# Two column tiles begun at a stage boundary, remainders last, and priority for the rows' transposes and splits

## The chip, the cores and the metric

The kernel runs on one core of a Trainium2 chip. The metric is the device time of one execution in microseconds (us). Three runs of the kernel before are shown, and one further execution was recorded by the profiler; span, windows and timelines are of that one. The engines are TensorE (PE, with its weight loads as PEld), VectorE (DVE), ScalarE (ACT), GpSimd (POOL) and SyncE (SP, which issues DMAs).

## The reference

One layer of a decoder step for a prompt of 1024 tokens (`D_MODEL` 1024) and for 8 sample rows with a paged cache of 8192 tokens each. The lines that the boundaries below compute:

```python
xp = xp + merge_heads(fox_prompt(q, k, v, logf), sgu_prompt(u, z, w_s[l], b_s[l]), ..., w_o[l])
xp = xp + cross_attend(rmsnorm(xp, g_cross[l]), mk, mv, w_cq[l], w_co[l])
f, conv_p = conv_ffn(rmsnorm(xp, g_ffn[l]), ..., w_up[l], conv_w[l], conv_b[l], w_down[l])
xp = xp + f
```

`cross_attend` begins with `xn @ w_cq`, `conv_ffn` with `xn @ w_up` (5632 columns). The sample rows go through the same layer, with attention over the cache (`fox_sample`).

## The kernel before

All data is float32. A product of two matrices is made of three matmuls per 128-row block of the contraction: each operand is split into a rounded part ("h") and a remainder ("l"), and `gemm3` (lines 268 to 274) issues h.h (L272), then the stationary h with the moving l (L273), then the stationary l with the moving h (L274). `split` makes the two parts: ACT copies (with a per-partition gain) into the rounded part (L238; L235 for weights), DVE subtracts it from the source for the remainder (L239; L236 for weights). `wload` fetches a piece of weight through SP and splits it; there are 4 raw buffers, 4 for remainders and 5 for rounded parts.

The prompt goes through the late stages in two halves of 512 tokens: merge and output projection, cross-attention, MLP. These are called mid0, ffn0, mid1 and ffn1 (`prompt`, L1830). At each of the two boundaries within a half the same thing happens:

- `out_proj` (L1014) multiplies by the last weight of the stage before (w_o, or w_co). It makes the first 512 columns of all four row blocks, then the second 512 columns in three groups: row block 0, row block 1, and row blocks 2 and 3 together (48 matmuls, L1072 to L1074). `residual` (L1002) adds each result to the rows `xt` on DVE (L1006) and sums its squares on ACT (L230). For row blocks 2 and 3 that already has the scheduler's priority (`HP`).
- Ahead of the MLP each row block is also scaled by its norm's factor: a factor on ACT (L1022) and POOL (L1023), the scaling on ACT (`scaled`, L1028, for row blocks 0 and 1; `both`, L1035 and L1036, for 2 and 3, with priority). Ahead of cross-attention the rows stay unscaled, and the factor is used later.
- `norm_T` (L1089) turns the rows into columns, in two passes: tokens of row blocks 0 and 1, then of 2 and 3. A pass has four tiles of four PE transposes (L1105) and two splits each (L238, L239). After each pass `first` is called, which multiplies the half that is there. Before the change that is one column tile of 128 outputs: 24 matmuls of 256 columns into one PSUM bank, held from the first pass to the end of the second.

`cross` (L1119) goes on with the other column tiles of w_cq at 512 columns each (`products`), `ffn` (L1250) with pairs of column tiles `ft` and `ft + NF` (NF is 22; gate and value), each with its own `wload` (`up`), then a convolution on ACT and DVE.

PSUM tiles come from `BK` (L146), which deals out a pool of four banks ("ba") and one of two ("bb") in turn. Rows, rounded parts and remainders of the prompt are tiles "u" of one pool of 18.

The sample rows run in the background: the generator `sample` is advanced by one step when the prompt's steps have yielded enough (`PACE`), except while `held` is set, which it is from the last group of `out_proj` to the end of `norm_T`. A step of the key side (`kstep`, L1403) gathers cache rows by a POOL DMA (L1406) into a "kv" buffer (4 of them), multiplies on DVE (L1422) and reduces (L1426). The value side is 16 matmuls (L1474) on a gathered buffer (L1468).

The order of instructions on each engine is fixed when the program is built. The context is opened with `schedule_with_timeline_sim=True`: a scheduler goes along a modelled timeline, and of the instructions that are ready it takes the one that was traced earliest. What is traced under `tc.high_priority()` is taken before everything else that is ready. `tc.issue_after` adds an order between two instructions of an engine. On the chip each engine then works through its list.

Of the kernel before, what the change touches and what calls it, by code (L numbers as in the profile page):

```python
# [18 lines left out]
P = 128  # L19
# [59 lines left out]
def build(nc, tc, ctx, a, phases=None):  # L79
# [66 lines left out]
    def BK():  # L146
        turn_[0] += 1
        return BB() if turn_[0] % BR == BR - 1 else BA()
# [83 lines left out]
    def split(src, h, l, scale=None):  # L232

        if scale is None:
            nc.scalar.activation(h, src, AF.Copy)  # L235
            nc.vector.tensor_tensor(l, src, h.bitcast(F32), op=ALU.subtract)  # L236
        else:
            nc.scalar.activation(h, src, AF.Copy, scale=scale)  # L238
            nc.vector.scalar_tensor_tensor(l, src, scale, h.bitcast(F32), op0=ALU.mult, op1=ALU.subtract)  # L239
# [28 lines left out]
    def gemm3(out, pairs):  # L268

        n = len(pairs)  # L270
        for i, (sh, sl, mh, ml) in enumerate(pairs):
            mmul(out, sh, mh, start=(i == 0), stop=False)  # L272
            mmul(out, sh, ml, start=False, stop=False)  # L273
            mmul(out, sl, mh, start=False, stop=(i == n - 1))  # L274

    paused = [False]

# [811 lines left out]
    def norm_T(ys, g0, first):  # L1089


        hs, ls = [], []
        for t0 in (0, 2):
            c = slice(t0 * P, (t0 + 2) * P)
            if callable(ys[t0]):
                ys[t0:] = ys[t0]()
            for kk in range(0, 8, 2):
                if t0 == 0:
                    h2, l2 = U([P, 2, 512], F32R), U([P, 2, 512], F32R)
                    hs += [h2[:, 0, :], h2[:, 1, :]]  # L1100
                    ls += [l2[:, 0, :], l2[:, 1, :]]
                tr = TR()
                for q in range(2):
                    for i in range(2):
                        nc.tensor.transpose(  # L1105
                            tr[:, (q * 2 + i) * P : (q * 2 + i + 1) * P], ys[t0 + i][:, (kk + q) * P : (kk + q + 1) * P], ident
                        )
                for q in range(2):
                    k = kk + q
                    split(tr[:, q * 256 : (q + 1) * 256], hs[k][:, c], ls[k][:, c], scale=gp[:, g0 + k : g0 + k + 1])  # L1110
                yield 0.6
            first(hs, ls, c)
            if t0 == 0:
                yield 3
        held[0] = False
        return hs, ls


    def cross(xt, sq):  # L1119
# [10 lines left out]
        fetch(1)  # L1130

        ws = [wload(wpair(a["w_cq"], kk, 0, 512), 1024) for kk in range(4)]
        q2, ps0 = [], MM()

        def products(out, ws, dt_, hs, ls, c):
            cb = slice(dt_ * P, (dt_ + 1) * P)
            gemm3(
                out,
                [(ws[k // 2][0][:, k % 2, cb], ws[k // 2][1][:, k % 2, cb], hs[k][:, c], ls[k][:, c]) for k in range(8)],
            )  # L1140

        hs, ls = yield from norm_T(xt, G_CROSS, lambda hs, ls, c: products(ps0[:, c], ws, 0, hs, ls, c))
# [61 lines left out]
        for n in range(2):  # L1204
            if n:
                ws = [wload(wpair(a["w_cq"], kk, n * 512, 512), 1024) for kk in range(4)]
            for dt_ in range(4):
                if dt_ % 2 == 0:
                    q2.append(U([P, 2, 512]))
                if n or dt_:  # L1210
                    ps = MM()
                    products(ps, ws, dt_, hs, ls, slice(0, 512))
                else:
                    ps = ps0
                nc.scalar.activation(q2[-1][:, dt_ % 2, :], ps[:, :512], AF.Copy)
# [32 lines left out]
    hlast = [const.tile([P, 2 * NF, 2], F32, tag=f"hlast{h}", name=f"hlast{h}") for h in range(2)]  # L1248

    def ffn(hf, xt, ys, late=None):  # L1250
        w0, pv0 = wload(a["w_up"][0], 1024), BK()

        def up(out, w, hs, ls, c):
            hv, lv = (w[q].rearrange("p (k c) -> p k c", c=P) for q in range(2))
            gemm3(out, [(hv[:, k, :], lv[:, k, :], hs[k][:, c], ls[k][:, c]) for k in range(8)])

        hs, ls = yield from norm_T(ys, G_FFN, lambda hs, ls, c: up(pv0[:, c], w0, hs, ls, c))
        if hf:

            fix = sm([P, 2 * NF, 2], "fix", 1)  # L1260
# [8 lines left out]
        for gi, gn in enumerate(GROUPS):  # L1269
            gh, gl = [], []  # L1270
            for f in range(f0, f0 + gn):
                hc2 = []
                for part in range(2):
                    ft = f + part * NF
                    cw = [gp[:, CW + i * 44 + ft : CW + i * 44 + ft + 1] for i in range(3)]
                    cb = gp[:, CB + ft : CB + ft + 1]
                    if ft:
                        w_, pv = wload(a["w_up"][ft], 1024), BK()
                        up(pv, w_, hs, ls, slice(0, 512))
                    else:  # L1280
# [730 lines left out]
```

## Time and profile before

| what | us |
|---|---|
| runs | 1814.82, 1810.97, 1816.68; median 1814.82 |
| the profiled execution | 1810.32 |
| its span, first to last instruction | 1808.3 |
| PE busy in it | 1741.4 |
| DVE busy | 1396.9 |
| ACT busy | 734.3 |

The granted clock of TensorE is 0.989 of the full one over the span. In a timeline a row has its start, its duration, engine, line of the kernel, operation, output and input, shapes and a count; in brackets stands how long the engine was idle just before, and what ended the idle time. Matmuls are pipelined: the distance from one start to the next is what one costs, and the duration is longer. In a table of waits a row has the waiting line, what released it, the sum, the number of times and the longest. "Busy" of PE counts time with a matmul in flight, at any clock.

### The profile page before, as it was taken

How to read it: one execution, taken by the hardware profiler on the slowest of the kernel's cores; microseconds unless marked ns; L12 is line 12 of the kernel's file. 1: busy time of each engine (PE TensorE's matmuls, PEld its weight loads, DVE VectorE, ACT ScalarE, POOL GpSimd, SP SyncE). 2: the span in 40 equal slices, each digit the busy share in tenths (PEclk: the TensorE clock that was granted, in tenths of full speed). 3: DMA queues.
4: the chain of work that ended last, by engine and by line, in shares of the span. 5: the costliest groups of instructions: out<-in, count | busy, mean ns of one | idle time of the engine just before them, and what ended most of it. 6: DMA issues, size and time to landing. Idle time of an engine off the chain costs nothing.

```text
span 1808.3 us, 25094 instructions
## 1 busy us (share of the span) xinstructions
PE 1741.4 (96%) x9637; PEld 1292.1 (71%) x9637; DVE 1396.9 (77%) x1729; ACT 734.3 (41%) x1378; POOL 501.8 (28%) x461
## 2 busy tenths in 40 slices
PE   8999999878999999999999999989999999999997
PEld 5887776656676767777777776766676678767875
DVE  4689658987788887999989899888875549855344
ACT  6332265465633544433323244235453333232332
POOL 1232333432133433223332233433322111001110
PEclk9999999998999999999999999999999999999999
DMA  7886888786597986778878788979878677568982
GB/s 290 304 304 230 293 316 331 261 278 196 213 404 268 346 315 252 264 280 338 321 278 317 267 313 329 383 285 349 325 283 314 246 289 253 183 260 295 358 314 81
DMA packets 157075, 521.06 MB, mean 288 GB/s; under 512 B 20875, under 2 KB 40843, under 8 KB 124187
## 3 DMA queue, kind: packets, MB, share of 16 engines
q0 software_dynamic: 57168, 341.14, 49.6%
q1 hardware_dynamic: 92874, 165.73, 26.2%
q10 hardware_dynamic: 6912, 12.59, 1.9%
q8 instruction: 76, 1.25, 0.3%
q14 instruction: 45, 0.36, 0.1%
HBM read 495.47 MB, written 23.93 MB: 287 GB/s over the span
## 4 chain that ended last, share of the span: by engine, by line
PE 53%; issue 8%; DMA 6%; DVE 5%; POOL 2%; ACT 2%; POOLq 0%; DVEq 0%; SPq 0%; ACTq 0%
PE ba L274 7%; PE ba L272 7%; PE ba L273 7%; PE bb L273 4%; PE bb L274 4%; PE bb L272 4%; PE dv L1474 4%; DMA kv<-cache_k,io 3%; DMA kv<-cache_v,io 2%; PE dv L321 1%; PE dv L1750 1%; PE ba L1055 1%; PE ba L1054 1%; PE ba L1056 1%; DVE s L1426 1%
## 5 line engine op out<-in xcount | busy, mean ns | idle before, releaser
L235 ACT ACTIVATE wh<-wr 128x1024 fp32r<-128x1024 f32 (+2 forms) x220 | 228.6, 1044 | 490.4 <-PE ba L273 157.7
L236 DVE TENSOR_TENSOR wl<-wr,wh 128x1024 fp32r<-128x1024 f32 (+2 forms) x220 | 262.3, 1198 | 174.0 <-PE ba L274 59.3
L1406 POOL DMA_INDIRECT kv<-cache_k,io x128 | 195.0, 1523 | 562.5 <-DVE s L1426 321.1
L1422 DVE TENSOR_TENSOR kv<-kv,d 128x1024 f32<-128x1024 f32 (+1 forms) x156 | 258.0, 1680 | 29.9 <-DMA kv<-cache_k,io 29.9
L1426 DVE TENSOR_REDUCE s<-kv 128x16 f32<-128x1024 f32 (+1 forms) x156 | 258.1, 1672 | 0.1
L1468 POOL DMA_INDIRECT kv<-cache_v,io x128 | 167.4, 1308 | 276.5 <-PE dv L1474 191.0
L273 PE MATMUL ba<-u,wh 128*128 128x512 f32 (+1 forms) x560 | 219.6, 392 | 1.8 <-DVE u L239 1.5
L272 PE MATMUL ba<-u,wh 128*128 128x512 f32 (+1 forms) x560 | 219.2, 393 | 1.7 <-ACT u L238 1.7
L274 PE MATMUL ba<-u,wl 128*128 128x512 f32 (+1 forms) x560 | 218.7, 392 | 0.0
L272 PE MATMUL ba<-wh,u 128*128 128x512 f32 (+1 forms) x495 | 186.9, 379 | 1.7 <-ACT u L235 1.7
L273 PE MATMUL ba<-wl,u 128*128 128x512 f32 (+1 forms) x495 | 185.5, 375 | 1.2 <-DVE wl L236 1.2
L274 PE MATMUL ba<-wh,u 128*128 128x512 f32 (+1 forms) x495 | 183.8, 376 | 0.0
L1474 PE MATMUL dv<-kv,s 128*32 128x512 f32 x1024 | 125.0, 598 | 2.9 <-DMA kv<-cache_v,io 2.9
L273 PEld LDWEIGHTS ba<-u,wh 128*128 128x128 f32 x560 | 106.0, 189 | 30.3 <-issue 5.2
L273 PE MATMUL bb<-u,wh 128*128 128x512 f32 (+1 forms) x304 | 118.6, 390 | 8.7 <-DVE u L239 8.7
L274 PEld LDWEIGHTS ba<-u,wl 128*128 128x128 f32 x560 | 105.9, 189 | 29.1 <-issue 6.1
L272 PEld LDWEIGHTS ba<-u,wh 128*128 128x128 f32 x560 | 105.9, 189 | 28.7 <-issue 4.0
L272 PE MATMUL bb<-u,wh 128*128 128x512 f32 (+1 forms) x304 | 118.5, 390 | 0.1
L274 PE MATMUL bb<-u,wl 128*128 128x512 f32 (+1 forms) x304 | 117.6, 387 | 0.0
L272 PEld LDWEIGHTS ba<-wh,u 128*128 128x128 f32 x495 | 93.0, 188 | 26.8 <-issue 6.9
L274 PEld LDWEIGHTS ba<-wh,u 128*128 128x128 f32 x495 | 92.8, 188 | 21.5 <-issue 3.8
L273 PEld LDWEIGHTS ba<-wl,u 128*128 128x128 f32 x495 | 93.1, 188 | 20.1 <-DVE wl L236 1.9
(432 smaller groups left out, 3251.0 us busy)
## 6 DMA issues: line engine op xcount, KB each, us to landing
wr<-w_up SPq DMA_DIRECT2D x88, 512.0 KB
kv<-w_up POOLq DMA_DIRECT2D x22, 1024.0 KB
wr<-w_down SPq DMA_DIRECT2D x40, 512.0 KB
kv<-w_down POOLq DMA_DIRECT2D x11, 1024.0 KB
wr<-w_in SPq DMA_DIRECT2D x16, 512.0 KB
wr<-w_o SPq DMA_DIRECT2D x16, 512.0 KB
wr<-w_cq SPq DMA_DIRECT2D x16, 512.0 KB
wr<-w_co SPq DMA_DIRECT2D x16, 512.0 KB
```

The costliest lines, as they stand in the source:

```text
L235: nc.scalar.activation(h, src, AF.Copy)
L236: nc.vector.tensor_tensor(l, src, h.bitcast(F32), op=ALU.subtract)
L272: mmul(out, sh, mh, start=(i == 0), stop=False)
L273: mmul(out, sh, ml, start=False, stop=False)
L274: mmul(out, sl, mh, start=False, stop=(i == n - 1))
L321: mmul(ps[32 * j : 32 * j + 32, :w], xT[:, k, :] if nk == 8 else xT[:, k * 8 : k * 8 + 32], raw[:, q, j * w : (j + 1) * w], start=(k == 0) ...
L1054: mmul(pss[i], mh[k][:, tb], wh, start=(k == korder[0]), stop=False)
L1406: nc.gpsimd.indirect_dma_start(kv, None, a["cache_k"], off(kidx[:, b, ch : ch + 1]))
L1422: nc.vector.tensor_tensor(kvv[:, i : i + m, :], kvv[:, i : i + m, :], qb.unsqueeze(1).broadcast_to((P, m, 512)), op=ALU.mult)
L1426: nc.vector.tensor_reduce(s[:, ch * 4 + i : ch * 4 + i + m, :].rearrange("p k h -> p (k h)"), kvv[:, i : i + m, :].rearrange("p k (h d) -> ...
L1468: nc.gpsimd.indirect_dma_start(kv, None, a["cache_v"], off(kidx[:, b, ch : ch + 1]))
L1474: mmul(dv[32 * j : 32 * j + 32, :], s[:, ch * 4 : ch * 4 + 4, :].rearrange("p k h -> p (k h)"), kvv[:, j, :], start=(ch == 1), stop=(ch == ...
```

## The change

Three things are changed. `gemm3_late` is new: it takes several products and issues for all of them first the matmuls that need the rounded part of the moving operand (h.h, and stationary l with moving h), and after these the ones that need its remainder. `first` in `cross` and in `ffn` now begins two column tiles and not one: tiles 0 and 1 of w_cq, and tiles 0 and 22 of w_up (whose second weight is loaded ahead of `norm_T`). The later loops skip what has been begun. And in `norm_T` the transposes and splits of both passes are traced under `tc.high_priority()`.

```diff
+    def gemm3_late(outs):
+
+        for out, pairs in outs:
+            for i, (sh, sl, mh, ml) in enumerate(pairs):
+                mmul(out, sh, mh, start=(i == 0), stop=False)
+                mmul(out, sl, mh, start=False, stop=False)
+        for out, pairs in outs:
+            for i, (sh, sl, mh, ml) in enumerate(pairs):
+                mmul(out, sh, ml, start=False, stop=(i == len(pairs) - 1))
...
                 tr = TR()
-                for q in range(2):
-                    for i in range(2):
-                        nc.tensor.transpose(
...
-                for q in range(2):
-                    k = kk + q
-                    split(tr[:, q * 256 : (q + 1) * 256], hs[k][:, c], ls[k][:, c], scale=gp[:, g0 + k : g0 + k + 1])
+                with tc.high_priority():
+                    for q in range(2):
+                        for i in range(2):
+                            nc.tensor.transpose(
...
+                    for q in range(2):
+                        k = kk + q
+                        split(tr[:, q * 256 : (q + 1) * 256], hs[k][:, c], ls[k][:, c], scale=gp[:, g0 + k : g0 + k + 1])
...
-        q2, ps0 = [], MM()
+        q2, begun = [], [MM() for _ in range(2)]
...
+        def first(hs, ls, c):
+            gemm3_late([(ps[:, c], pairs(ws, d, hs, ls, c)) for d, ps in enumerate(begun)])
+
+        hs, ls = yield from norm_T(xt, G_CROSS, first)
...
-                if n or dt_:
+                if n or dt_ >= len(begun):
                     ps = MM()
-                    products(ps, ws, dt_, hs, ls, slice(0, 512))
+                    gemm3(ps, pairs(ws, dt_, hs, ls, slice(0, 512)))
                 else:
-                    ps = ps0
+                    ps = begun[dt_]
...
-        w0, pv0 = wload(a["w_up"][0], 1024), BK()
+        begun = {ft: (wload(a["w_up"][ft], 1024), BK()) for ft in (0, NF)}
...
+        def first(hs, ls, c):
+            gemm3_late([(pv[:, c], pairs(w, hs, ls, c)) for w, pv in begun.values()])
+
+        hs, ls = yield from norm_T(ys, G_FFN, first)
...
-                    if ft:
+                    if ft in begun:
+                        pv = begun.pop(ft)[1]
+                    else:
                         w_, pv = wload(a["w_up"][ft], 1024), BK()
-                        up(pv, w_, hs, ls, slice(0, 512))
-                    else:
-                        pv = pv0
+                        gemm3(pv, pairs(w_, hs, ls, slice(0, 512)))
```

More of the change, by code (lines that the diff above doesn't have):

```diff
@@ L1102, in norm_T @@
                 tr = TR()
-                for q in range(2):
-                    for i in range(2):
-                        nc.tensor.transpose(
-                            tr[:, (q * 2 + i) * P : (q * 2 + i + 1) * P], ys[t0 + i][:, (kk + q) * P : (kk + q + 1) * P], ident
-                        )
-                for q in range(2):
-                    k = kk + q
-                    split(tr[:, q * 256 : (q + 1) * 256], hs[k][:, c], ls[k][:, c], scale=gp[:, g0 + k : g0 + k + 1])
+                with tc.high_priority():
+                    for q in range(2):
+                        for i in range(2):
+                            nc.tensor.transpose(
+                                tr[:, (q * 2 + i) * P : (q * 2 + i + 1) * P], ys[t0 + i][:, (kk + q) * P : (kk + q + 1) * P], ident
+                            )
+                    for q in range(2):
+                        k = kk + q
+                        split(tr[:, q * 256 : (q + 1) * 256], hs[k][:, c], ls[k][:, c], scale=gp[:, g0 + k : g0 + k + 1])
                 yield 0.6
@@ L1132, in cross, with pairs @@
         ws = [wload(wpair(a["w_cq"], kk, 0, 512), 1024) for kk in range(4)]
-        q2, ps0 = [], MM()
-        def products(out, ws, dt_, hs, ls, c):
+        q2, begun = [], [MM() for _ in range(2)]
+        def pairs(ws, dt_, hs, ls, c):
             cb = slice(dt_ * P, (dt_ + 1) * P)
[L1137 to L1142, printed above, removed]
+            return [(ws[k // 2][0][:, k % 2, cb], ws[k // 2][1][:, k % 2, cb], hs[k][:, c], ls[k][:, c]) for k in range(8)]
+        def first(hs, ls, c):
+            gemm3_late([(ps[:, c], pairs(ws, d, hs, ls, c)) for d, ps in enumerate(begun)])
+        hs, ls = yield from norm_T(xt, G_CROSS, first)
         r = rows_rstd(sq, 0, 4)
@@ L1250, in ffn, with pairs @@
     def ffn(hf, xt, ys, late=None):
-        w0, pv0 = wload(a["w_up"][0], 1024), BK()
-        def up(out, w, hs, ls, c):
+        begun = {ft: (wload(a["w_up"][ft], 1024), BK()) for ft in (0, NF)}
+        def pairs(w, hs, ls, c):
             hv, lv = (w[q].rearrange("p (k c) -> p k c", c=P) for q in range(2))
-            gemm3(out, [(hv[:, k, :], lv[:, k, :], hs[k][:, c], ls[k][:, c]) for k in range(8)])
-        hs, ls = yield from norm_T(ys, G_FFN, lambda hs, ls, c: up(pv0[:, c], w0, hs, ls, c))
+            return [(hv[:, k, :], lv[:, k, :], hs[k][:, c], ls[k][:, c]) for k in range(8)]
+        def first(hs, ls, c):
+            gemm3_late([(pv[:, c], pairs(w, hs, ls, c)) for w, pv in begun.values()])
+        hs, ls = yield from norm_T(ys, G_FFN, first)
         if hf:
```

## The prediction

> **What bounds the kernel now.** I read the page first, then the waits of TensorE over the part that the change can touch, then the windows of the four boundaries, and last the timelines inside them. A boundary here is a call of norm_T: into cross-attention (cross) and into the gated MLP (ffn), once for each half of the prompt.
>
> ```profile
> span 1808.3 us, 25094 instructions
> PE 1741.4 (96%) x9637; PEld 1292.1 (71%) x9637; DVE 1396.9 (77%) x1729; ACT 734.3 (41%) x1378; POOL 501.8 (28%) x461
> ...
> PE bb L273 <- DVE u L239: 8.7, 5, 5.5
> ...
> PE ba L272 <- ACT u L238: 1.7, 3, 0.9
> ...
> PE ba L273 <- DVE u L239: 1.5, 1, 1.5
> ...
> PE ba L1105 <- ACT u L1035: 1.1, 1, 1.1
> ```
>
> TensorE (PE) is busy 96% of the span, so only its idle 67 us and the time it runs at a lower clock can be won without taking work away. Between 500 and 1400 us its longest waits are the four lines above: a product with the remainder waits for the remainder's subtraction (L273 for L239), a product for the rounded part (L272 for L238), a transpose for a scaled row (L1105 for L1035). All belong to the boundaries. The windows (columns: length, PE busy, PEld, DVE, ACT, POOL, granted clock, DMA share, GB/s) give the sums: in order cross 0, ffn 0, cross 1, ffn 1, and then the three stretches with a low clock.
>
> ```profile
> core 0: us, PE busy (x) PEld busy (x) DVE busy (x) ACT busy (x) POOL busy (x), PEclk, DMA share, GB/s
> 545.00:565.00 20.00, 17.27 (x115) 13.78 (x114) 19.24 (x32) 9.07 (x22) 5.68 (x5) 0.91 0.92 362
> 702.00:718.00 16.00, 12.61 (x75) 10.60 (x74) 11.90 (x26) 12.38 (x31) 3.80 (x4) 0.89 0.95 385
> 1177.00:1204.00 27.00, 20.96 (x133) 16.13 (x132) 24.90 (x36) 9.78 (x22) 10.51 (x8) 0.87 0.73 263
> 1340.00:1359.00 19.00, 17.45 (x118) 14.79 (x120) 11.14 (x23) 12.23 (x30) 1.35 (x3) 1.00 0.39 159
> ...
> 559.00:564.00 5.00, 4.63 (x22) 3.75 (x21) 5.00 (x8) 0.47 (x1) 0.11 (x1) 0.66 1.04 409
> 705.00:714.00 9.00, 6.15 (x33) 5.55 (x34) 5.67 (x14) 7.27 (x19) 2.11 (x3) 0.81 1.01 421
> 1188.00:1195.00 7.00, 5.89 (x29) 5.89 (x30) 6.23 (x12) 1.55 (x4) 2.49 (x2) 0.54 0.47 159
> ```
>
> Idle: 2.73 + 3.39 + 6.04 + 1.55 = 13.7 us. Lost to the clock, as busy time times the missing share: 4.63 x 0.34 + 6.15 x 0.19 + 5.89 x 0.46 = 1.6 + 1.2 + 2.7 = 5.5 us. Together **19.2 us** is all that the boundaries hold.
>
> Why PE stands is seen in the largest gap, first PE and then VectorE (DVE):
>
> ```profile
> 1177.48 0.39 PE L1074 MATMUL ba<-wh,u 128*128 128x512 f32 x1
> ...
> 1180.59 0.60 PE L1105 MATMUL bb<-cp,u 128*128 128x128 f32 x4
> 1181.03 1.04 PE L1105 MATMUL ba<-cp,u 128*128 128x128 f32 x8
> ...
> 1189.11 0.58 PE L273 MATMUL bb<-u,wh 128*128 128x256 f32 x1 [5.50 <-DVE u L239]
> ```
>
> ```profile
> 1167.33 0.68 DVE L1006 TENSOR_TENSOR u<-bb,u 128x512 f32<-128x512 f32 x1
> ...
> 1177.22 1.39 DVE L1006 TENSOR_TENSOR u<-ba,u 128x512 f32<-128x512 f32 x2 [1.03 <-PE ba L1074]
> ...
> 1184.41 0.86 DVE L239 SCALAR_TENSOR_TENSOR u<-ba,gp,u 128x256 fp32r<-128x256 f32 x2
> 1185.19 1.20 DVE L1426 TENSOR_REDUCE s<-kv 128x16 f32<-128x1024 f32 x1
> 1186.32 2.35 DVE L1422 TENSOR_TENSOR kv<-kv,d 128x1024 f32<-128x1024 f32 x2
> 1188.59 0.47 DVE L239 SCALAR_TENSOR_TENSOR u<-ba,gp,u 128x256 fp32r<-128x256 f32 x1
> ```
>
> The background's key products (L1422, L1426) stand in DVE's order ahead of the remainder that PE wants, for 3.4 us here (1185.19 to 1188.59). They were traced before norm_T, so the scheduler preferred them. And the rows are there early: row block 1 is complete at 1168.0, 9.5 us before the last out_proj matmul at 1177.48, yet its transposes come after that matmul, because they are traced after it.
>
> The gain counts one for one only if the prompt's own work ends last. It does:
>
> ```profile
> 1783.66 0.31 SPq L1804 DMA_DIRECT2D o_ys<-vsum  x1
> 1795.25 8.61 SPq L1340 DMA_DIRECT2D o_y<-u  x5
> ```
>
> The background's last store is issued at 1783.7, the prompt's last around 1803.9.
>
> **The change part by part.** *Priority.* Each boundary has 32 transposes, 16 L238 and 16 L239. None is added or removed. The transposes of the first two row blocks can now run inside the last group of out_proj, 9.5 us earlier at cross 1. The PE time of a transpose is 0.11 us start to start (1180.59 to 1181.03 for four), so 16 of them take 1.8 us out of the boundary and put it into out_proj: zero in sum. Their splits, 0.43 us each on DVE (0.86 for two at 1184.41) and about as much on ScalarE (ACT), run beside out_proj's matmuls, which fill 11 us of that group (48 at 0.23 us). If that cover were gone, 8 splits would cost 8 x 0.43 = 3.4 us. What is delayed instead is background: 16 x 0.43 = 6.9 us of DVE per boundary go ahead of key products. These hold their kv buffers longer, so POOL's next gathers start later; nobody on the prompt's path reads them, and dense stages follow.
>
> *Two tiles, remainders last.* The first half's products are now 48 matmuls of 256 columns instead of 24. Their spacing:
>
> ```profile
> 563.43 0.28 PE L272 MATMUL bb<-u,wh 128*128 128x256 f32 x1
> ...
> 564.50 0.39 PE L272 MATMUL bb<-u,wh 128*128 128x512 f32 x1
> 564.73 0.40 PE L273 MATMUL bb<-u,wh 128*128 128x512 f32 x1
> ```
>
> Nine of 256 columns lie between 563.43 and 564.50, 0.119 us each; one of 512 takes 0.23. So the first half is 48 x 0.119 = 5.7 us of cover where there was 2.85, and 32 of the 48 need no remainder. The price: 24 products of 512 become 48 of 256, 24 x (0.238 - 0.23) = 0.2 us per boundary, **0.8 us** for four. No matmul is added otherwise; the second tile is only begun earlier, and both banks are held until the second half is through. That leaves four of six banks for transposes, of which at most four tiles per half are asked for: taken as nothing, at worst one split's wait of 0.9 us per tile.
>
> *Chain of the second half, cross.* PE is through with out_proj at 1177.7 (1177.48 and one spacing of 0.23); the sums of rows 2 and 3 end at 1177.22 + 1.39 = 1178.6. Transposes for one split 0.4, eight splits at 0.43, the last subtraction 0.4: 1178.6 + 4.3 = 1182.9. PE has 5.7 + 1.8 us of its own from 1177.7, to 1185.2, before it needs all of them. Nothing waits unless DVE is 2.3 us late; I leave 0.5 us at each cross boundary.
>
> *Chain of the second half, ffn.* Here rows 2 and 3 must still be scaled:
>
> ```profile
> 692.45 1.15 ACT L1028 ACTIVATE u<-u,fac 128x1024 f32<-128x1024 f32 x1 [1.63 <-POOL fac L1023]
> ...
> 706.82 1.32 ACT L1035 ACTIVATE u<-u,fac 128x512 f32<-128x512 f32 x2
> ...
> 710.87 1.34 ACT L1036 ACTIVATE u<-u,fac 128x512 f32<-128x512 f32 x2
> ```
>
> ```profile
> core 0: us, ACT busy (x), PEclk, DMA share, GB/s
> ...
> 702.00:718.00 16.00, 6.50 (x16) 0.89 0.95 385
> ```
>
> The row just above is the window of ffn 0 for L238 alone: 6.50 / 16 = 0.41 us each. Row 1 is scaled at 693.6, so the first half again fits inside out_proj, which ends at 702.2. The second ends at 712.2, 10 us after it; eight L238 of the first half stood among these instructions on ACT, and without them it is some 8 x 0.41 = 3.3 us earlier, 6.7 us after. Then come 3.4 us of splits, 10.1 us, against 5.7 + 1.8 = 7.5 us of PE work plus products that follow each split. I leave 1.5 us at ffn 0 and 0.8 at ffn 1.
>
> *DMAs.* Only the load of w_up tile 22 is traced earlier, ahead of norm_T instead of behind it; on SP's queue it was the next weight anyway, and it passes only the background's small loads. Its split is now ahead of norm_T too: at most 1.2 us of DVE during out_proj's matmuls.
>
> *Clock.* The dip to 0.66 follows a gap of 2.04 us:
>
> ```profile
> 558.67 0.39 PE L273 MATMUL bb<-u,wh 128*128 128x256 f32 x1 [2.04 <-DVE u L239]
> ```
>
> With the long gaps the dips go at both cross boundaries (4.3 us); at ffn 0, where 1.5 us may stay, I count half (0.6). The Trainium skill (TensorE: Matmul & The Clock Gate, Part 1) has the clock halve only after an idle window of about 3.4 us. By that rule cross 0 would have lost nothing and the sum below would be 1.6 us smaller, 10.9; the trace has the dip, and the trace decides.
>
> *New waits.* A transpose placed early may wait for a row sum that DVE has late, with out_proj's matmuls behind it. The trace of before shows no such wait. Bounds: nothing (the sum of row 1 was done 9.5 us ahead), and what DVE itself can be held up ahead of that sum:
>
> ```profile
> DVE kv L1422 <- DMA kv<-cache_k,io: 23.2, 15, 3.9
> DVE wl L236 <- PE ba L274: 17.5, 6, 5.0
> ```
>
> Up to 5.0 us for a weight buffer. I take 0.5 us per boundary, near the lower end, because ahead of the sum at 1177.22 DVE had waited 1.03 us for PE, and not the other way round. A gain below nothing is excluded: PE does not stop there today.
>
> **Sum.** Idle 13.7 - (0.5 + 1.5 + 0.5 + 0.8) = 10.4; clock 4.9; less 0.8 and 4 x 0.5 = 2.0: **12.5 us**. The profiled execution took 1810.3 us (span 1808.3 and 2 around it), so 1797.8. The median of the runs shown is 1814.8, 4.5 us above it, and the forecast for a median is 1814.8 - 12.5 = **1802.3 us**.
>
> **The rivals.** *The priority does little.* DVE cannot break off an instruction, and a split whose L238 is not done lets a key product in (1.2 us). Then only the two tiles help: 32 products without remainders, 3.8 us, lie over the gaps. Of 5.5 us 3.8 go, of the 2.04 all, little at ffn: about 6 us idle and 1 to 2 of clock, 1807.5. For it: the order is written from a modelled timeline, not the real one. Against: the 3.4 us at 1185.19 are three instructions in a row, of which a preferred split needs to let in one.
>
> *The gap moves.* The early transposes wait 2.3 to 5.0 us per boundary; 9.1 to 19.9 us in all eat the 14.5 us to within 5.4. Time about 1815.
>
> *Slower.* The same place, the last group of out_proj, at a higher price: an early transpose waits for L1006, which stands on DVE behind a weight split that waits 5.0 us for its buffer and two key products (2.3 us), 7.3 us per boundary. Four of these are 29 us against 14.5: 1829.5. It decides from 5.0 us per boundary on. For it: both waits are in the trace, and in-order PE has 48 matmuls behind the transpose. Against: the same buffer is freed by PE's matmuls of this group, so the scheduler cannot place such a transpose ahead of them. The Trainium skill (same page, Part 2, Step-by-step) has matmuls start and complete in program order; nothing in this trace overtakes either.
>
> **How the numbers follow.** Forecast 0.52; priority does little 0.12; gap moves 0.16; slower 0.20. A difference of 0.3%, 5.4 us, is about what a measurement of this kernel can tell from no change. Faster by more 0.52 + 0.12 = 0.64, within 0.16, slower 0.20. The range's lower end is all 19.2 us, 1795.6, less the runs' scatter of some 3.8 us (1811.0 to 1814.8): 1792. The upper end is the sum with 5.0 us waited at each boundary, 15.3 - 0.8 - 20 = -5.5: 1820. It leaves out the slower case.
>
> **What would show it.** Right: first-half transposes (L1105) among out_proj's L1072 to L1074; no L1422 or L1426 between two L239 of one half; PE's waits for L239 under 2 us in sum; clock above 0.97 in all four windows; the stretches shorter by 12 to 15 us together. Wrong: PE waits at L1105 for L1006 or L1028 inside out_proj, new waits at L1474 for cache_v, or idle PE later in cross-attention, which would mean that a new order gave back what the boundaries gained.

## The result, and the profile after

Ten runs of the kernel after have a median of 1808.57 us (1805.43 to 1812.79), ten of the kernel before on the same chip 1816.21 (1809.38 to 1821.46). The ratio is 0.997, with a 95% interval of 0.9958 to 0.9982: **5.4 us faster, between 3 and 8**. The medians alone lie 7.6 us apart, which the interval holds too; what follows goes by the ratio. The forecast was 12.5 us. The profiled execution took 1805.43 us, the shortest of the ten. Their granted clock goes from 0.986 (1812.52 us) to 0.994 (1806.19 us), 0.991 in the profiled one: what is said below of single clock dips (stretches at half clock) holds for one execution.

The page of the kernel after: the same DVE time to a tenth, 96 more matmuls, 2.1 us less of PE.

```profile
span 1803.7 us, 25307 instructions
...
PE 1739.3 (96%) x9733; PEld 1291.7 (72%) x9733; DVE 1396.9 (77%) x1729; ACT 734.1 (41%) x1378; POOL 500.8 (28%) x461
```

The windows of the four boundaries, as long as those of before and moved with the end of out_proj (columns: length, busy of PE, PEld, DVE, ACT, POOL, granted clock, DMA share, GB/s):

```profile
core 0: us, PE busy (x) PEld busy (x) DVE busy (x) ACT busy (x) POOL busy (x), PEclk, DMA share, GB/s
546.00:566.00 20.00, 20.00 (x150) 17.33 (x149) 19.82 (x34) 6.82 (x15) 4.80 (x5) 1.00 0.80 293
702.00:718.00 16.00, 14.06 (x109) 13.04 (x108) 9.73 (x22) 10.44 (x25) 2.12 (x3) 1.00 0.83 341
1180.00:1207.00 27.00, 24.31 (x168) 20.71 (x168) 24.90 (x33) 8.75 (x18) 11.14 (x8) 1.00 0.88 328
1332.00:1351.00 19.00, 16.85 (x126) 14.11 (x119) 13.45 (x28) 11.03 (x26) 6.05 (x5) 1.00 0.68 268
```

Length less PE's time is the idle time: 0 + 1.94 + 2.69 + 2.15 = 6.8 us where there were 13.7, and the clock is full in all four, where 5.5 us were lost before. The boundaries won 6.9 + 5.5 = **12.4 us**, less 0.8 for the narrower matmuls. So the forecast gain was there, and more than half of it is gone at the end. PE's waits from 500 us on show where:

```profile
PE dv L1488 <- DMA kv<-cache_v,io: 7.1, 3, 2.9
PE ba L1208 <- ACT u L1201: 3.1, 3, 1.4
PE bb L281 <- DVE wl L236: 2.7, 1, 2.7
PE ba L272 <- DVE t L1300: 2.4, 1, 2.4
PE ms L1473 <- DVE dg L1466: 2.0, 1, 2.0
...
PE ba L280 <- ACT u L238: 1.2, 1, 1.2
PE ba L1116 <- ACT u L1046: 0.7, 1, 0.7
```

(L1488 is the value matmul, L1474 before; L1208 the attention's product with the values of the memory; L281 the stationary remainder in `gemm3_late`; L1116 the transposes.) The waits for L239 (8.7 and 1.5 us before) are gone. The waits for cache_v were there before, the second line of the same table:

```profile
PE dv L1474 <- DMA kv<-cache_v,io: 2.9, 4, 1.2
```

Outside the boundaries PE's idle times from cross 0's out_proj on, added up from the brackets of the timeline, went from 10.9 to 15.5 us, and the clock lost 3.7 us more there, nearly all of it in two new dips at 793 and 1547 us. The sum, with the 1.5 us by which the stretch ahead of cross 0 happened to be shorter: -12.4 + 0.8 + 4.6 + 3.7 - 1.5 = -4.8; the spans differ by 4.6.

By halves of the prompt (from the first out_proj matmul of cross 0 to the last tile's evacuation in ffn 0), before and after:

```profile
496.40:1093.70 597.30, 588.03 (x2845) 436.44 (x2844) 536.33 (x556) 234.32 (x420) 195.01 (x130) 0.99 0.81 305
```

```profile
494.90:1092.00 597.10, 587.60 (x2892) 436.27 (x2891) 536.57 (x559) 234.98 (x419) 188.71 (x130) 1.00 0.81 306
```

**The first half kept nothing**: 597.3 and 597.1 us, although its two boundaries hold 4 us less idle time and the clock is full there. What is left comes from the second half, 714.6 to 711.7.

How the time goes back is seen at the value matmuls in ffn 0. POOL's second gather of a pair and the matmuls that use it, first before, then after:

```profile
790.70 0.94 POOL L1468 DMA_INDIRECT kv<-cache_v,io  x1 [3.77 <-PE dv L1474]
```

```profile
797.98 1.92 PE L1474 MATMUL dv<-kv,s 128*32 128x512 f32 x16 [0.30 <-DMA kv<-cache_v,io]
```

```profile
785.28 0.94 POOL L1482 DMA_INDIRECT kv<-cache_v,io  x1 [2.17 <-PE dv L1488]
```

```profile
793.10 2.52 PE L1488 MATMUL dv<-kv,s 128*32 128x512 f32 x12 [2.43 <-DMA kv<-cache_v,io]
```

The data took 7.3 and 7.8 us from issue to use. The gather can only be issued when the pair of matmuls ahead of it has released its buffer (the brackets of the POOL rows name it). In the order before, PE came to the matmuls 7.0 us behind the issue, in the order after 5.4 us behind it (793.10 - 2.43 - 785.28): less of the prompt's work stands between the two pairs. PE works its list in order, so all of the prompt's matmuls behind them waited 2.43 us, and the clock dipped on top.

### The profile page after: what moved, and what is told of

It is laid out like the page before. It is cut to its first block, busy times and chain, and to the rows that moved or that the text cites. A ratio compares the mean times of both kernels' runs of the same rounds, so it can differ in the third digit from the quotient of the medians.

```text
span 1803.7 us, 25307 instructions
## 1 busy us (share of the span) xinstructions
PE 1739.3 (96%) x9733; PEld 1291.7 (72%) x9733; DVE 1396.9 (77%) x1729; ACT 734.1 (41%) x1378; POOL 500.8 (28%) x461
## 4 chain that ended last, share of the span: by engine, by line
PE 50%; issue 10%; DMA 9%; DVE 8%; ACT 2%; POOL 2%; POOLq 0%; DVEq 0%; ACTq 0%; SPq 0%
PE ba L272 6%; PE ba L274 6%; PE ba L273 6%; DMA kv<-cache_v,io 5%; PE dv L1488 4%; PE bb L272 3%; PE bb L274 3%; PE bb L273 3%; DVE wl L236 1%; DMA kv<-cache_k,io 1%; DVE kv L1436 1%; DVE s L1440 1%; DMA wr<-w_o 1%; PE dv L331 1%; PE dv L1764 1%
## 5 line engine op out<-in xcount | busy, mean ns | idle before, releaser
L235 ACT ACTIVATE wh<-wr 128x1024 fp32r<-128x1024 f32 (+2 forms) x220 | 229.2, 1045 | 462.3 <-PE ba L273 147.8
L236 DVE TENSOR_TENSOR wl<-wr,wh 128x1024 fp32r<-128x1024 f32 (+2 forms) x220 | 263.2, 1202 | 176.4 <-PE ba L274 56.9
L1420 POOL DMA_INDIRECT kv<-cache_k,io x128 | 188.2, 1471 | 555.3 <-DVE s L1440 296.6
L1436 DVE TENSOR_TENSOR kv<-kv,d 128x1024 f32<-128x1024 f32 (+1 forms) x156 | 258.3, 1683 | 17.9 <-DMA kv<-cache_k,io 17.7
L1482 POOL DMA_INDIRECT kv<-cache_v,io x128 | 171.6, 1341 | 288.6 <-PE dv L1488 187.8
L272 PE MATMUL ba<-u,wh 128*128 128x512 f32 x512 | 203.5, 398 | 0.0
L274 PE MATMUL ba<-u,wl 128*128 128x512 f32 x512 | 202.3, 396 | 0.0
L273 PE MATMUL ba<-u,wh 128*128 128x512 f32 x512 | 202.2, 395 | 0.0
L273 PE MATMUL ba<-wl,u 128*128 128x512 f32 (+1 forms) x495 | 185.5, 376 | 1.3 <-DVE wl L236 1.3
L274 PE MATMUL ba<-wh,u 128*128 128x512 f32 (+1 forms) x495 | 183.4, 377 | 0.0
L1488 PE MATMUL dv<-kv,s 128*32 128x512 f32 x1024 | 128.5, 605 | 7.1 <-DMA kv<-cache_v,io 7.1
L272 PEld LDWEIGHTS ba<-u,wh 128*128 128x128 f32 x512 | 96.2, 188 | 29.6 <-issue 8.6
L274 PEld LDWEIGHTS ba<-u,wl 128*128 128x128 f32 x512 | 96.1, 188 | 27.2 <-issue 4.8
L273 PEld LDWEIGHTS ba<-u,wh 128*128 128x128 f32 x512 | 96.2, 188 | 24.2 <-issue 3.1
L273 PEld LDWEIGHTS ba<-wl,u 128*128 128x128 f32 x495 | 93.7, 189 | 20.5 <-issue 2.1
L274 PEld LDWEIGHTS ba<-wh,u 128*128 128x128 f32 x495 | 93.1, 188 | 20.3 <-issue 2.9
L272 PE MATMUL bb<-u,wh 128*128 128x512 f32 x256 | 102.0, 398 | 0.0
L274 PE MATMUL bb<-u,wl 128*128 128x512 f32 x256 | 101.9, 398 | 0.0
L273 PE MATMUL bb<-u,wh 128*128 128x512 f32 x256 | 101.0, 395 | 0.0
```

The lines of the kernel that those rows point to most:

```text
L1420: nc.gpsimd.indirect_dma_start(kv, None, a["cache_k"], off(kidx[:, b, ch : ch + 1]))
L1436: nc.vector.tensor_tensor(kvv[:, i : i + m, :], kvv[:, i : i + m, :], qb.unsqueeze(1).broadcast_to((P, m, 512)), op=ALU.mult)
L1482: nc.gpsimd.indirect_dma_start(kv, None, a["cache_v"], off(kidx[:, b, ch : ch + 1]))
L1488: mmul(dv[32 * j : 32 * j + 32, :], s[:, ch * 4 : ch * 4 + 4, :].rearrange("p k h -> p (k h)"), kvv[:, j, :], start=(ch == 1), stop=(ch == ...
```

## The experiments

Theory G: the boundaries won what was forecast, and about 7 us were given back elsewhere, because the priority pushes background work back. Rival S: the boundaries themselves won half. Later the question became whether the loss belongs to the change (P) or to the one order that was dealt (L). Ratios are to runs of the kernel before on the same chip, 95% intervals in brackets.

**Parts of the change.** The tiles without the priority, and the priority alone in the kernel before:

```diff
-                with tc.high_priority():
+                with nullcontext():
```

> The change without the priority: two column tiles begun and remainders last, transposes and splits in traced order. Theory G (the boundaries gave the forecast 12.5 us, and some 8 of it was given back later, by waits of TensorE for the background's cache_v gathers and the clock dips behind them, because the priority pushes background work back): the boundaries still hold 6 to 9 us of idle time, but nothing is given back, so 4 to 7 us faster than before, as much as the whole change. Rival S (the boundaries themselves gave only 5 to 6 us, and the priority is what gave it): within 2 us of before.

> The priority alone on the kernel before: one column tile, remainders in their old place. Theory G: 8 to 10 us less idle time and clock loss at the boundaries, 5 to 8 given back, so 1 to 4 us faster. Rival S: as the whole change, 5 to 6 us faster, with no new waits for cache_v.

Tiles alone: 1814.44 us, ratio 1.0010 [0.9989, 1.0031]. Priority alone: 1809.51 us, 0.9984 [0.9971, 0.9997], 2.9 us faster. In time the first went as S said, the second as G. But the boundaries' idle time fell in both, to 8.3 us (tiles) and 9.0 (priority) from 13.7, so S's reason did not hold. Nor did G's: from 500 us on PE has no wait for cache_v left with the priority alone (2.9 us before) and 3.9 us of it with the tiles alone, and outside the boundaries the priority alone has 10.1 us of idle time (10.9 before) and 3.5 us more lost to the clock. So these runs do not show that it is the priority that brings the waits for cache_v. The tiles alone have 12.6 us more idle time elsewhere, 9.1 of them at one place in the attention of the second half:

```profile
1256.25 1.06 ACT L235 ACTIVATE wh<-wr 128x1024 fp32r<-128x1024 f32 x1 [4.82 <-DMA wr<-w_co]
...
1257.69 0.59 ACT L1167 ACTIVATE t<-ba 128x512 f32<-128x512 f32 x1
```

```profile
1258.34 5.36 PE L1180 MATMUL ba<-t,u 128*128 128x256 f32 x16 [9.10 <-ACT t L1167]
```

```profile
1249.77 2.35 DVE L1436 TENSOR_TENSOR kv<-kv,d 128x1024 f32<-128x1024 f32 x2
1252.04 1.22 DVE L236 TENSOR_TENSOR wl<-wr,wh 128x1024 fp32r<-128x1024 f32 x1
```

```profile
1253.32 2.59 SPq L249 DMA_DIRECT2D wr<-w_co  x2
```

Read backwards: PE waits 9.1 us for a copy on ACT (L1167), which stands behind a weight's rounding (L235), which waits for the load of w_co. Two of those loads are issued only at 1253.32, when the subtraction at 1252.04, which frees a raw buffer, is through; and ahead of it on DVE stand key products. So one order made a chain over four queues that another does not have.

**Without the cache_v wait.** In both kernels the value matmuls read a constant tile, so the use of cache_v is left out, and the sample rows' attention does not come out right:

```diff
-                            kvv[:, j, :],
+                            rmask,
```

> The kernel before, with the value products of the cache attention (16 matmuls a step) reading a constant tile in place of the gathered rows; the gathers are still issued. It leaves out the use of cache_v, so TensorE can never wait for those gathers. Theory G: 2 to 5 us faster than before (its 2.9 us of such waits go). Rival S: the same, it only is the base for the next run.

> The changed kernel with the same cut: value products read a constant tile, gathers still issued. Theory G: without waits for cache_v the whole 12.5 us of the boundaries come through, so 10 to 13 us faster than the previous run of this list. Rival S, or a loss that has nothing to do with cache_v: 5 to 6 us faster than the previous run, as with the gathers read.

1860.51 us, 1.0262 [1.0242, 1.0282], and 1819.43, 1.0035 [1.0018, 1.0051]. Neither theory expected that. Taking the dependency away let the scheduler re-deal everything: in the first, idle PE at the boundaries rose to 26.3 us; with the change it is 9.8. As a test of the wait this failed. In this order the change is worth 41 us; the boundaries, with the clock counted in, went from 43.4 to 14.9 us, 28.5 us less.

**Halves.** The change where `phase[0]` is mid0 or ffn0 alone, and where it is mid1 or ffn1 alone; elsewhere one tile, `gemm3`, no priority:

```diff
+        on = phase[0] in ('mid0', 'ffn0')
-        q2, begun = [], [MM() for _ in range(2)]
+        q2, begun = [], [MM() for _ in range(2 if on else 1)]
...
-                with tc.high_priority():
+                with tc.high_priority() if phase[0] in ('mid0', 'ffn0') else nullcontext():
```

> The change is made in the first half of the prompt alone (cross 0 and ffn 0); cross 1 and ffn 1 run as in the kernel before. Theory G (each boundary wins what was forecast, and the re-laid background gives a part back soon behind it): the two boundaries hold under 2.5 us of idle PE, and mid0 and ffn0 together end within 2 us of the kernel before, so 0 to 2 us faster in all. Rival S (the boundaries themselves win only half): the two boundaries still hold 4 us or more, and what they win, 2 to 4 us, is kept to the end.

> The change is made in the second half of the prompt alone (cross 1 and ffn 1). Theory G: the order of the first 1100 us is that of the kernel before; cross 1 and ffn 1 win about 6 us and lose some 2 us in ffn1: 3 to 5 us faster. Rival S: 2 to 3 us faster, with 3 us or more of idle PE left at cross 1. A third possibility is that the first half and the second half do not add up to the whole, because the order of everything behind a boundary is dealt anew.

First half alone: 1816.7 us, 1.0025 [1.0006, 1.0043], 4.5 us slower, which neither theory expected. The two boundaries hold 1.95 us of idle time, as G said. Second half alone: 1809.14, 0.9981 [0.9967, 0.9994], 3.4 us faster, the time that G gave; cross 1 holds 0.3 us there, but ffn 1 holds 5.2, of which 4.2 are one wait for cache_v. The two halves together would be 1.1 us slower than before, and the whole change is 5.4 us faster: the parts do not add up, which the expectation of the second one had allowed for. The first half's windows and its longest wait:

```profile
498.70:1095.70 597.00, 587.36 (x2892) 436.07 (x2891) 536.43 (x559) 234.53 (x420) 191.48 (x130) 1.00 0.81 305
```

```profile
PE dv L1496 <- DMA kv<-cache_v,io: 7.4, 3, 2.6
```

597.0 us where the whole change has 597.1 and before 597.3. The waits for cache_v stand at the same places as in the kernel after (627 and 797 us; there 624 and 793, 4 us earlier as the start is) with 2.6 and 2.3 us for 2.9 and 2.4. Up to 1162 us PE has the order of the kernel after here, so with the same order these waits recur in another execution. They need not: in the run e17 below PE has the order of the kernel after from 61 to 769 us, and there it does not wait for cache_v at this place but, a little later, for a copy on ACT, with a dip of 6.8 us behind:

```profile
633.21 6.63 PE L1208 MATMUL ba<-u,t 128*128 128x512 f32 x8 [3.35 <-ACT u L1201]
```

What recurs in all three is 4 to 5 us of idle PE in this attention (2.5 before); which wait takes them differs. And from 1095.7 us to the end, with the source of before, the kernel with the first half alone takes 1818.0 - 1095.7 = 722.3 us against 714.6: 7.7 us worse, with nothing changed in that half but what stood ahead of it.

**An earlier gather.** The kernel after with the two value gathers traced ahead of the same step's key gather, throughout (e7) and only from mid0 on (e9), and the latter in the kernel before (e10):

```diff
+            more = values(g) if phase[0][:3] in ("mid", "ffn") else None
             left = 1
             if b < 8:
                 left = yield from kstep(b, ch, st[b])
...
-                pend += [vstep(vb, c, st[vb], dv[vb]) for c in (vch - 1, vch)]
+            if more is None:
+                more = values(g)
+            pend += more
```

> The kernel after, with the two value gathers of a background step traced ahead of that step's key gather, so that POOL issues them one key gather (about 1 to 2 us) earlier. Theory G, cache_v part: the value matmuls' waits for cache_v (7.1 us in the profile after) fall to under 3 us, and the kernel is 2 to 4 us faster than the kernel after, 8 to 10 faster than the kernel before. Rival: the waits fall, yet the time stays within 2 us of the kernel after, since the late stretch is lost elsewhere (the key gathers come later and DVE's key products crowd other places). A rise of the waits would refute that the lead of the gather sets them.

> The kernel after, with the two value gathers of a background step traced ahead of that step's key gather only from mid0 on, so that the first 490 us are unchanged. Theory G, cache_v part: the 2.43 us wait at the value matmuls in ffn0 and its clock dip go, so the stretch from tile 11 to tile 22 of ffn0 takes 109 us again and not 113; waits for cache_v under 3 us in all; 3 to 5 us faster than the kernel after, 8 to 10 faster than the kernel before. Rival (re-dealt order): the waits at these places go, others come, and the time is within 3 us of the kernel after or slower.

> The same move of the value gathers in the kernel before, whose waits for cache_v are 2.9 us. Theory G: within 3 us of the kernel before, and the distance to the kernel above is 8 to 12 us, since the boundaries' gain is then kept. Rival: it moves by more than 3 us in either direction, as any new order does.

e7: 1843.77 us, 1.0167 [1.0144, 1.019]; some 25 us are lost ahead of 521 us, where the change is not. e9: 1814.67, 1.0008 [0.9993, 1.0023]. e10: 1819.78, 1.0038 [1.0023, 1.0053]. At the place itself e9 did what was expected. The stretch of ffn 0 from tile 11 to tile 22, in the kernels before, after and e9:

```profile
785.30:894.60 109.30, 109.00 (x523) 79.20 (x522) 104.81 (x93) 36.28 (x56) 41.75 (x27) 1.00 0.87 328
```

```profile
779.90:893.00 113.10, 110.67 (x523) 79.58 (x522) 104.85 (x93) 36.53 (x56) 43.64 (x27) 0.98 0.83 313
```

```profile
783.70:892.80 109.10, 109.10 (x523) 79.23 (x523) 103.38 (x90) 37.46 (x58) 44.17 (x25) 1.00 0.89 334
```

That one wait with its dip costs 4 us, and an earlier gather takes it away. But others came up in the two attentions, and the kernel became slower; in its table of waits:

```profile
PE dv L1488 <- DMA kv<-cache_v,io: 6.2, 2, 5.5
PE ba L1200 <- ACT u L1188: 5.8, 1, 5.8
```

The rival expected it; G's 3 to 5 us did not come. In the kernel before the same move costs 6.9 us (e10), as the rival said, although PE does not wait for cache_v there at all from 500 us on.

**Three passes.** All h.h matmuls first, then those with the stationary remainder, then the rest:

```diff
                 mmul(out, sh, mh, start=(i == 0), stop=False)
+        for out, pairs in outs:
+            for i, (sh, sl, mh, ml) in enumerate(pairs):
                 mmul(out, sl, mh, start=False, stop=False)
```

> The kernel after, with the begun tiles' matmuls in three passes (all h.h, then all with the stationary remainder, then all with the moving remainder). In the profile after PE waits 2.69 us at cross 1 for the remainder of a weight of w_cq, at the second kind of matmul; with 16 matmuls of h.h (1.9 us) ahead of it 0 to 1 us of that wait is left. If only that wait moves: 1.5 to 2.5 us faster than the kernel after. If the order behind the boundary is dealt anew and that decides, it comes out anywhere within 5 us on either side, with the boundary itself better.

1810.53 us, 0.9987 [0.9972, 1.0001]. The boundary cross 1 did get better, 0.7 us idle and not 2.7. Behind it the order was dealt anew, ffn 1 went from 2.2 to 3.2 us, waits for cache_v grew from 7.1 to 8.6 us, and nothing is left.

**Other orders with the same work.** One number is changed, in the kernel after and in the kernel before: how many microseconds the prompt must yield before the background advances a step.

```diff
-PACE = {... 'mid0': 8.0, 'ffn0': 8.5, ...}
+PACE = {... 'mid0': 8.1, 'ffn0': 8.5, ...}
```

> The kernel after with the background's pace in mid0 at 8.1 instead of 8.0: the same work, one per cent later in mid0, and a new order on every engine from some 600 us on. If the payback is a fixed cost of the priority: within 1.5 us of the kernel after. If it is the lot of one order among many: 2 to 8 us off in either direction, with the four boundaries as short as in the kernel after and other waits behind them.

> The same in the kernel before. If a new order alone is worth little: within 1.5 us of the kernel before. If it is worth as much as what the change lost: 2 to 8 us off. The difference between this run and the one above estimates the change once more with another order behind it: 8 to 14 us if the boundaries' 12.5 us are what is kept on the whole, 3 to 7 if a payback of some 7 us belongs to the change.

> The kernel after, with the background's pace in mid0 at 7.9 instead of 8.0: the same work in another order. Both theories: 2 to 10 us off the kernel after; the four boundaries hold under 8 us of idle PE.

> The same in the kernel before; the boundaries hold 11 us or more. What counts is the distance to the run above. Theory P (priority pays back about 7 us through later gathers, whatever the order): 3 to 8 us. Theory L (the boundaries' 12.5 us are won in every order, and what lies outside them is dealt anew each time, with a mean of nothing): anywhere from 2 to 25 us, and a mean over this pair, the two others and the first ones of 10 to 15 us.

> The kernel after with the pace in mid0 at 8.2. Both theories: 2 to 10 us off the kernel after; the four boundaries hold under 8 us of idle PE.

> The same in the kernel before; the boundaries hold 11 us or more. Theory P: 3 to 8 us above the run before this one. Theory L: 2 to 25 us, with the mean over all pairs at 10 to 15 us.

> The kernel after, with the background's pace in ffn0 at 8.6 instead of 8.5, so that everything up to ffn0 keeps its order. Both theories: within 6 us of the kernel after, with cross 0 and ffn 0 unchanged.

> The same in the kernel before. Theory P: 3 to 8 us above the run before this one. Theory L: the loss in the first half (some 7 us of 9) stays, as the order there stays, and the second half is dealt anew: 0 to 15 us above.

Ratios to the kernel before, and what the two profiles of each pair hold, from cross 0's out_proj to the end: idle time of PE plus time by the clock's missing share, from the last out_proj matmul to the second evacuated tile of the next stage ("boundaries"), and everywhere else. (A dip in which PE also stands is counted in both, so the sums do not add up to the last microsecond.)

| order | ratio without the change | with it | the change | boundaries, us | elsewhere, us |
|---|---|---|---|---|---|
| as given | 1 | 0.9970 | -0.30% | 20.5 to 6.8 | 14.0 to 22.3 |
| mid0 at 8.1 (e12, e11) | 1.0066 | 0.9948 | -1.18% | 22.4 to 3.3 | 27.5 to 21.8 |
| mid0 at 7.9 (e14, e13) | 1.0008 | 0.9950 | -0.58% | 16.7 to 7.8 | 25.0 to 30.6 |
| mid0 at 8.2 (e16, e15) | 1.0028 | 0.9992 | -0.36% | 17.9 to 4.2 | 25.0 to 29.4 |
| ffn0 at 8.6 (e18, e17) | 0.9986 | 0.9957 | -0.29% | 20.0 to 5.6 | 14.6 to 25.2 |
| earlier gathers (e10, e9) | 1.0038 | 1.0008 | -0.30% | 30.2 to 9.1 | 17.8 to 34.8 |

A ratio in the table has an interval of some 0.0013 to 0.0025 to either side. Three things follow. A new order alone moves the kernel before by -0.1 to +0.7%, as much as the change does. The boundaries win in every order, 9 to 21 us, 15 in the mean. And elsewhere 4 to 17 us are lost in five orders of six, 6.7 in the mean; in one, 5.7 are won, and there the change is worth 20 us (1825.49 to 1805.38). The last pair but one kept PE's order up to some 770 us: 7.0 us between its medians, which both P and L allow. P had said 3 to 8 us in every pair; four of six are within it, and one is 21 us by the ratios, outside all that had been expected of it. L had said 10 to 15 us in the mean; it is 9 (by the medians 5 to 8 us in five orders, 20 in one). So neither holds as it stood: a loss outside goes with the change **in most orders**, as P has it, and its size is dealt anew each time, from +17 to -6, as L has it. Each of these sums is of one execution.

The windows of the four boundaries in e12 and e11, the pair with the largest difference, with the whole stretch as the last row:

```profile
545.50:571.70 26.20, 22.95 (x133) 18.50 (x133) 22.34 (x36) 9.38 (x23) 6.09 (x6) 0.87 0.82 312
707.80:733.00 25.20, 23.91 (x139) 19.09 (x138) 17.11 (x30) 17.53 (x38) 4.09 (x5) 0.93 0.52 199
1192.10:1223.30 31.20, 25.14 (x153) 19.44 (x152) 29.13 (x40) 10.05 (x23) 10.35 (x9) 0.89 0.79 281
1353.40:1379.40 26.00, 24.39 (x146) 20.04 (x145) 16.09 (x29) 17.06 (x37) 3.98 (x5) 0.93 0.51 194
496.50:1821.00 1324.50, 1284.85 (x6975) 949.89 (x6973) 1019.02 (x1203) 490.64 (x910) 353.52 (x295) 0.99 0.78 291
```

```profile
552.30:572.50 20.20, 20.20 (x155) 17.72 (x154) 20.02 (x33) 6.97 (x16) 4.12 (x5) 1.00 0.75 274
703.40:721.80 18.40, 16.52 (x134) 14.54 (x132) 11.48 (x24) 12.59 (x30) 2.28 (x4) 1.00 0.44 161
1182.40:1200.50 18.10, 17.64 (x140) 15.34 (x139) 17.04 (x25) 6.85 (x16) 6.74 (x6) 1.00 0.83 306
1337.00:1361.00 24.00, 23.07 (x165) 19.58 (x163) 13.82 (x28) 13.68 (x30) 2.06 (x4) 1.00 0.46 183
500.30:1805.70 1305.40, 1278.00 (x7071) 944.91 (x7069) 1018.48 (x1203) 491.71 (x910) 345.62 (x295) 0.99 0.79 295
```

The last rows have the same DVE and ACT time to about 1 us, and lengths that differ by 19 us: only the order of the waits.

**A version that is faster.** Three of these lie below both kernels: e17 with 0.9957 [0.9943, 0.9971], e13 with 0.9950 [0.9934, 0.9966], e11 with 0.9948 [0.9924, 0.9971], 8 to 9 us faster than before. Their intervals lie below 1 and overlap that of the change as given (0.9958 to 0.9982): they beat the kernel before, and whether they beat the kernel after is not shown. They are also the best of several orders, so part of their lead can be the luck of the pick.

## Why the prediction was wrong in size

The direction was right; 12.5 us were forecast and 5.4 came. By its steps:

- **What bounds the kernel**: the four lines are not the longest waits between 500 and 1400 us. Second in that table stands the wait for cache_v with 2.9 us, and 1.6 us of L934 for L239 and 1.2 of L274 for L236 are longer than the last line shown. The wait that mattered afterwards was left out of the reading.
- **Priority, transposes**: right. They run among out_proj's matmuls at cross 1, without a wait.

```profile
1171.79 0.40 PE L1084 MATMUL ba<-wh,u 128*128 128x512 f32 x1
1172.03 0.27 PE L1116 MATMUL ba<-cp,u 128*128 128x128 f32 x1
1172.05 0.48 PE L1082 MATMUL ba<-wh,u 128*128 128x512 f32 x1
...
1176.17 0.60 PE L1116 MATMUL ba<-cp,u 128*128 128x128 f32 x4
```

- **New waits**, 2.0 us: too dear. Only the 0.7 us at L1116 for L1046, at ffn 0, is of that kind.
- **What is left at the boundaries**, 0.5 + 1.5 + 0.5 + 0.8 = 3.3 us: 6.8. Cross 0 holds nothing and ffn 0 1.9. At cross 1 it is 2.69 and not 0.5: the remainder of a weight of w_cq, which no step of the sum had, is behind two key products on DVE.

```profile
1183.73 2.36 DVE L1436 TENSOR_TENSOR kv<-kv,d 128x1024 f32<-128x1024 f32 x2
1186.00 1.23 DVE L236 TENSOR_TENSOR wl<-wr,wh 128x1024 fp32r<-128x1024 f32 x1
```

```profile
1187.29 0.39 PE L281 MATMUL bb<-u,wl 128*128 128x256 f32 x1 [2.69 <-DVE wl L236]
```

At ffn 1 2.05 of the 2.15 us are the background's: L1473 waits for its softmax (L1466).
- **Clock**, 4.9 of 5.5 us: all 5.5 won in this execution. Over the boundaries alone the sum is 12.4 - 0.8 = 11.6 us, against 12.5.
- **The step that failed** is the sentence on what is delayed: "POOL's next gathers start later; nobody on the prompt's path reads them, and dense stages follow", priced at nothing. The value matmuls read them, and they stand in PE's one list with the prompt's matmuls behind them. The term for what a new order does behind the boundaries was nothing; 8.3 us more were lost elsewhere in this order (14.0 to 22.3; 6.7 in the mean of six orders), of them 4.2 in longer waits for cache_v (2.9 to 7.1) and 3.7 in dips. The last sentence of the prediction had named the two signs, new waits for cache_v and idle PE later in cross-attention, and given them no price. That it is the delay of the gathers by the priority that brings the loss is not shown: the priority alone left no such wait.
- **The rivals.** "The priority does little" gave nearly the right time, 1807.5, by luck and for a wrong reason: priority alone brings the boundaries from 13.7 to 9.0 us. "The gap moves" put 9 us or more of waits at the early transposes, where there are 0.7. "Slower" did not happen.

What stays open is a single cause of the loss elsewhere. Waits for cache_v rise in three pairs of six (2.9 to 7.1 us as given, 4.5 to 6.4 in e12 and e11, none to 6.2 in e10 and e9), stay in one (4.4 and 4.5 in e18 and e17) and fall in two (2.7 to 2.0 in e14 and e13, 7.2 to 5.5 in e16 and e15); the attention's own chain on ACT takes part as well. That DVE, 96% busy in the stretch of ffn 0 shown above, has no room into which the displaced key products could go would be a reason; it was not tested.

## What to carry to other kernels

Background work is not off the path as long as its instructions stand in the same in-order list as the main work: a new order can move a wait to the next place where the two meet. In this kernel some 7 of the 15 us won at the boundaries were lost elsewhere, in the mean of six orders. Where a scheduler deals the order, judge a change of half a per cent by the stretch it touches and by several orders: a change of pace by about one per cent moved the same kernel by 0.7%. And when a gap has been closed, look at once for the same time in the idle brackets of the next stretch.

## What the runs showed of the hardware

The clock dips start on a grid of 3.41 us that is fixed within an execution, whatever the gap's own place, and last whole cells of it at half speed: one or two in the kernels before and after from 500 us on, up to five in other runs. That is so for all dips between 200 us and the last matmul in the 20 traces of this case. In the kernel before, dips start at 559.58, 709.77 and 1187.63 us, 44 and 184 times 3.413 us after the first. Windows of one cell each, in the kernel before, then after:

```profile
556.17:559.58 3.41, 1.37 (x8) 0.97 (x7) 3.41 (x7) 1.42 (x3) 1.00 (x1) 1.00 1.01 404
559.58:562.99 3.41, 3.04 (x10) 2.23 (x9) 3.41 (x6) 0.00 (x0) 0.00 (x0) 0.50 1.04 401
```

```profile
619.36:622.77 3.41, 1.41 (x4) 0.34 (x2) 3.41 (x5) 2.35 (x8) 1.25 (x1) 1.00 1.00 387
622.77:626.18 3.41, 2.55 (x22) 1.11 (x23) 1.66 (x3) 0.56 (x5) 0.94 (x1) 1.00 0.97 354
790.02:793.43 3.41, 0.98 (x7) 0.34 (x9) 3.40 (x4) 1.65 (x3) 0.00 (x0) 1.00 1.01 420
793.43:796.84 3.41, 3.41 (x17) 0.88 (x10) 0.88 (x1) 0.00 (x0) 1.03 (x2) 0.50 1.00 419
```

2.04 and 2.43 us of idle time inside one cell were followed by a cell at 0.50. The gap of 2.86 us that ended at 623.63 left 2.00 us in one cell and 0.86 in the next, and none followed; nor after the 2.69 us at 1187.29, which straddle two cells as well. So of two gaps alike one costs 1.7 us more than the other, by where it falls. The first gap shown, 2.04 us ahead of L273 at cross 0, stands in the run with the second half alone with 2.05 us, and no dip follows there.

How much idle time a cell needs is not a fixed figure. In all 20 traces a full-clock cell with more than 2.00 us of it was followed by a dip, but in e12 one with 1.22 us was, too, none of it longer than 0.5 us at a stretch:

```profile
710.01:713.42 3.41, 2.19 (x10) 1.39 (x10) 1.81 (x5) 3.41 (x12) 1.11 (x2) 1.00 0.97 398
713.42:716.83 3.41, 3.41 (x14) 3.11 (x15) 3.06 (x9) 3.41 (x8) 1.01 (x1) 0.50 0.05 20
```

What else decides is open. The Trainium skill (TensorE: Matmul & The Clock Gate, Part 1) has a free-running window of 3413 ns, and the grid agrees; that a window has to be idle as a whole, as its table of states can be read, does not: 1.22 to 2.43 of its 3.41 us were enough here.
